# Stick-breaking attention: queries as rows, cumulative sums by a reversed scan

## The chip, the cores and the metric

The kernel runs on one NeuronCore of a Trainium2 chip. The metric is the device time of one execution in microseconds; shown below are the median of three timed runs and one execution taken with the hardware profiler. The engines are TensorE (PE, with its weight loads as PEld), VectorE (DVE), ScalarE (ACT), GpSimd (POOL) and SyncE (SP); TensorE reads SBUF and writes PSUM, an accumulator memory of eight banks, from which VectorE and ScalarE copy. "L955" means line 955 of the kernel before.

## The reference

A two-layer decoder trunk on 512 tokens of width 1024, all float32. Layer 0 mixes a gated linear recurrence with forgetting attention, layer 1 a recurrent branch (Griffin: causal convolution, gates, RG-LRU) with stick-breaking attention. After each mixer stand a residual with LayerNorm, a SwiGLU feed-forward and a second LayerNorm. The change is in the stick-breaking attention of layer 1: 8 heads of 64, blocks of 128 queries.

```python
z = einsum('bqhd,bkhd->bhqk', q_block, k[:, :q1]) * scale
mask = kpos < qpos                                    # strictly causal
log_one_minus = where(mask, log_sigmoid(-z), 0.0)
suffix = cumsum(log_one_minus, axis=3, reverse=True) - log_one_minus
log_w = log_sigmoid(z) + suffix
w = where(mask, exp(log_w), 0.0)
out = einsum('bhqk,bkhd->bqhd', w, v[:, :q1])
```

So each weight needs a sum over all later keys of the same query. With softplus(z) = -log_sigmoid(-z), and since log_sigmoid(z) = z - softplus(z), a weight is exp(z minus the sum of softplus over this key and all later allowed ones).

## The kernel before

Large products are made to nearly float32 accuracy out of three float32r products: each operand is split into a high part (a ScalarE copy) and a low part (a VectorE subtraction), and `mm3` (L256 to L258) issues high by high, high by low and low by high. `weights` (L238 to L246) loads a 128x1024 weight block over SP's queue and splits it; `proj` runs one block of a projection, 24 matmuls of 512 columns, into one of two PSUM banks with the tag "g"; `put` (L251, L252) splits a result.

The order is not written by hand. The kernel is traced in program order, and a planner orders the instructions of each engine by priority and its own costs, assigns buffers of a tag in turn, and inserts semaphores; each engine then runs its queue in order. `high_priority` moves weight splits ahead, `issue_after` and `behind` add an order between two instructions.

Layer 1 (`layer1`) runs the recurrent branch (`griffin`), the value projection, and then four times `sb_pair`, each for two heads e = 0, 1. After the last pair is traced, `out_rows(yc, S_WO1)` runs the half of the output projection that needs only the recurrent branch; the other half follows in the next phase with all four pairs' results.

`qk_pair` projects queries and keys of a pair, head 0 on partitions 0 to 63 and head 1 on 64 to 127. A head's tile holds its high part on its own half of the partitions; on the other half the queries hold their low part (L732), and the keys a second copy of the high part, which VectorE casts out of PSUM (L737). With the low part of the keys in `kz` (L738, zero on the other half), two products give the scores to three terms: q high and low by k high, and q high by k low.

`sb_pair` has keys as rows: for each key block j it computes scores of all queries from block j on, with k as stationary and q as moving operand, and adds a mask by a third product with `sbmask`. The 8 blocks of a pair (2 heads, j = 0 to 3, 512 - 128 j queries wide) are packed into five tiles of 512 columns. Per tile:

- ScalarE copies the scores out of PSUM (L937), VectorE clips them (L938), ScalarE takes exp and ln(1 + x) (L939, L940), VectorE the maximum with z (L941): softplus.
- The softplus is split for TensorE: high part `sh` (L943), low part `sl` (L944).
- The sum over later keys runs down the partitions, so TensorE makes it (L955): `ntri` (-1 on and below the diagonal) sums within the key block, `none` (all -1) adds the later key blocks of the same head, each for `sh` and `sl`, into one bank.
- VectorE adds scores and sums (L957), ScalarE takes the exponential (L958). Keys are rows, so the weights are the moving operand of the value products (L966) as they stand.

A pair has 34 products L955 and 16 products L966. Tags and their numbers of buffers: z 6, l 4, sh 5, sl 5, qk 7. `griffin` uses buffers of sh for its input gates and of sl for its GeLU gates before the pairs need them.

For comparison, `fox_pair` in layer 0 already has queries as rows, transposes its weights on TensorE and stores them in a tile `pT`.

Of the kernel before, what the change touches and what calls it, by code (L numbers as in the profile page):

```python
# [15 lines left out]
P = 128  # L16
# [40 lines left out]
class Trunk:  # L57
    def __init__(self, tc, ctx, ins, out):
# [7 lines left out]
        tile_("fill", [P, 64])  # L66
# [7 lines left out]
        tile_("ntri", [P, P], F32R)  # L74
        tile_("none", [P, P], F32R)
# [640 lines left out]
    def qk_pair(self, iq, ik, low, high=None):  # L716
# [18 lines left out]
        for e, d in enumerate(hv):  # L735
            nc.scalar.copy(ks[e][d], kp[d])
            nc.vector.tensor_copy(ks[e][hv[1 - e]], kp[d])  # L737
            nc.vector.tensor_tensor(low[e][d], kp[d], ks[e][d].bitcast(F32), ALU.subtract)  # L738
# [87 lines left out]
    def griffin(self, xr):  # L826
# [29 lines left out]
        st = []  # L856
        for j in range(4):
# [14 lines left out]
            ig = self.t2k("ig", tag="sh")  # L872
# [4 lines left out]
        gts = []  # L877
        for j in range(4):
            ps = self.proj(S_GR + j)
            g = self.t2k("gt", tag="sl")  # L880
            A(g, ps, AF.Gelu_apprx_tanh)
            gi = self.newest()
            gts.append(g)
# [4 lines left out]
        for j in range(4):  # L888
# [18 lines left out]
            nc.vector.tensor_tensor(ix, ix, gts[j], ALU.mult)  # L907
# [6 lines left out]
    def sb_pair(self, hp, v):  # L914
# [6 lines left out]
        tiles = (((0, 3, 384), (0, 1, 0)), ((1, 3, 384), (1, 1, 0)), ((0, 2, 0), (1, 2, 256)), ((0, 0, 0),), ((1, 0, 0),))  # L921
        sp = {}
        for parts in tiles:
            z, l = self.t2k("z", tag="z"), self.t2k("l", tag="l")
            for e in (0, 1):
                mine = [p for p in parts if p[0] == e]
                if not mine:
                    continue
                ps = self.bank("s", "z")
                for _, j, o in mine:  # L930
                    n = T - j * P
                    b = slice(j * P, j * P + P)
# [4 lines left out]
                nc.scalar.copy(z[:, c], ps[:, c])  # L937
# [4 lines left out]
            sh, sl = self.t2k("sh", dt=F32R, tag="sh"), self.t2k("sl", dt=F32R, tag="sl")  # L942
            nc.scalar.copy(sh, l)  # L943
            nc.vector.tensor_tensor(sl, l, sh.bitcast(F32), ALU.subtract)  # L944
            for e, j, o in parts:
                sp[e, j] = (sh, sl, o)
            sp[parts] = z
        for ti, parts in enumerate(tiles):
            z = sp[parts]
            ps = self.bank(("pt", "po")[ti % 2], "cu")  # L950
            lo = [(self.none, sp[e, i], o + (i - j) * P, T - i * P) for e, j, o in parts for i in range(j + 1, NTB)]
            mms = [(self.ntri, sp[parts[0][:2]][:2] + (0,), 0, T)] + lo
            for n, (w, (sh, sl, oi), c, m) in enumerate(mms):
                for x in (sh, sl):
                    nc.tensor.matmul(ps[:, c:c + m], w, x[:, oi:oi + m], start=n == 0 and x is sh,  # L955
                                     stop=n == len(mms) - 1 and x is sl)
            nc.vector.tensor_tensor(z, z, ps, ALU.add)  # L957
            A(z, z, AF.Exp)  # L958
            ex = self.newest()

        at = {(e, j): (sp[parts], o) for parts in tiles for e, j, o in parts}
        for j in range(NTB):
            for e in range(2):
                h = 2 * hp + e
                z, o = at[e, j]
                nc.tensor.matmul(po[64 * e:64 * e + 64, j * P:T], v[j][:, h * 64:h * 64 + 64], z[:, o:o + T - j * P],  # L966
                                 start=j == 0, stop=j == NTB - 1)
                if j == 0 and e == 0:
                    self.behind(self.newest(), ex)
# [3 lines left out]
    def layer1(self, xr):  # L973
# [3 lines left out]
        for e in range(2):  # L977
            self.nc.gpsimd.memset(self.kz[e][64 - 64 * e:P - 64 * e].bitcast(F32), 0.0)
        yc = self.griffin(xr)
# [13 lines left out]
def hybrid_trunk_kernel(ctx: ExitStack, tc: tile.TileContext, out, **ins):  # L993
# [9 lines left out]
    with t.phase("l1", v=4, qk=7, kz=2, z=6, l=4, sh=5, sl=5) as t.ph:  # L1003
# [38 lines left out]
def layout(inp):  # L1042
# [40 lines left out]
    cst = np.zeros((P, 4, P), f)  # L1083
    cst[:, 0, :] = np.eye(P)
    cst[:, 1, :] = np.where(r[None, :] > r[:, None], -1e30, 0)
    cst[:, 2, :] = np.where(r[:, None] >= r[None, :], -1e30, 0)
    cst[:, 3, :] = np.where(r[:, None] >= r[None, :], -1, 0)
# [25 lines left out]
```

## Time and profile before

| | us |
|---|---|
| median of 3 runs (1236.01 to 1238.81) | 1237.58 |
| the profiled execution | 1234.23 |
| its span, first to last instruction | 1232.5 |
| TensorE busy / weight loads | 1211.2 / 984.2 |
| VectorE busy | 760.5 |
| ScalarE busy | 522.3 |
| GpSimd busy | 66.1 |
| mean granted TensorE clock | 0.995 |

Times in rows of the profile are microseconds from the start of the span unless marked ns. A group's row gives line, engine, operation, "out<-in" by tile names, shapes, count, then busy time with the mean of one, and the idle time of that engine just before with what ended most of it. In the order of time a row is start, recorded length, instruction. [...] A wait's row gives who waited for whom: total, times, longest.

### The profile page before, as it was taken

Reading aid. Unit: us, or ns where it says so; the run is one execution under the profiler, and the core shown is the slowest. Engines: PE = TensorE matmul, PEld = TensorE weight load, DVE = VectorE, ACT = ScalarE, POOL = GpSimd, SP = SyncE. Lnnn points to the kernel's source line nnn. Section 1 sums busy time; section 2 is a strip of 40 time slices with the busy share of each in tenths; the row PEclk is TensorE's granted clock in tenths of the full one; section 3 lists DMA queues with packets and bytes.
Section 4 is the critical chain, followed back from the end, with each engine's and each line's share of the span. In section 5 each row is a group of like instructions: output and inputs, shape, how many; then the busy total and the mean of one; then the engine's idle time right before and its main releaser. Section 6 shows DMA issues by size and latency. Waiting matters only on the chain.

```text
span 1232.5 us, 15454 instructions
## 1 busy us (share of the span) xinstructions
PE 1211.2 (98%) x6119; PEld 984.2 (80%) x6119; DVE 760.5 (62%) x1157; ACT 522.3 (42%) x794; POOL 66.1 (5%) x81
## 2 busy tenths in 40 slices
PE   9999999999999999999999998999999999999997
PEld 6787777679888888888889776777988888888886
DVE  7638789769355635464387597686844554456346
ACT  7447567433233323332233757683333433333220
POOL 2000000000002000200000000000000200020001
PEclk9999999999999999999999999999999999999999
DMA  6421211134637433742324231102554643374321
GB/s 243 154 71 51 86 53 52 52 120 123 219 86 120 137 99 89 119 133 90 103 88 135 69 88 50 45 25 86 157 188 99 103 144 96 91 115 137 103 69 69
DMA packets 45895, 128.03 MB, mean 104 GB/s; under 512 B 4592, under 2 KB 6000, under 8 KB 45824
## 3 DMA queue, kind: packets, MB, share of 16 engines
q1 hardware_dynamic: 35568, 108.51, 27.6%
q0 software_dynamic: 8960, 16.81, 8.6%
q10 hardware_dynamic: 1296, 1.73, 0.4%
q8 instruction: 48, 0.79, 0.3%
q14 instruction: 23, 0.19, 0.1%
HBM read 124.90 MB, written 2.10 MB: 103 GB/s over the span
## 4 chain that ended last, share of the span: by engine, by line
PE 90%; DVE 6%; ACT 2%; DMA 1%; issue 1%; SPq 0%; DVEq 0%; ACTq 0%
PE pf L257 13%; PE pf L256 13%; PE pf L258 13%; PE pj L257 5%; PE pj L256 5%; PE pj L258 5%; PE po L258 4%; PE po L256 4%; PE po L257 4%; PE fa L256 2%; PE fa L258 2%; PE fa L257 2%; PE sc L643 1%; PE fc L258 1%; PE fc L257 1%; PE fc L256 1%
## 5 line engine op out<-in xcount | busy, mean ns | idle before, releaser
L245 ACT CAST wh<-ws 128x1024 fp32r<-128x1024 f32 x143 | 150.2, 1051 | 309.1 <-PE pf L257 119.1
L246 DVE TENSOR_TENSOR wl<-ws,wh 128x1024 fp32r<-128x1024 f32 x143 | 174.9, 1223 | 155.2 <-ACT wh L245 150.4
L256 PE MATMUL pf<-xh,wh 128*128 128x512 f32 x640 | 249.0, 389 | 0.0
L257 PE MATMUL pf<-xl,wh 128*128 128x512 f32 x640 | 249.0, 389 | 0.0
L258 PE MATMUL pf<-xh,wl 128*128 128x512 f32 x640 | 249.0, 389 | 0.0
L257 PEld LDWEIGHTS pf<-xl,wh 128*128 128x128 f32 x640 | 120.1, 188 | 25.1
L258 PEld LDWEIGHTS pf<-xh,wl 128*128 128x128 f32 x640 | 120.1, 188 | 24.9
L256 PEld LDWEIGHTS pf<-xh,wh 128*128 128x128 f32 x640 | 120.1, 188 | 24.7
L533 DVE TENSOR_TENSOR s<-s,pf 128x512 f32<-128x512 f32 x44 | 30.3, 688 | 147.9 <-PE pf L258 147.9
L256 PE MATMUL pj<-xh,wh 128*128 128x512 f32 x256 | 104.2, 407 | 1.0 <-DVE qk L732 0.9
L257 PE MATMUL pj<-xl,wh 128*128 128x512 f32 x256 | 103.6, 405 | 0.2 <-DVE xl L252 0.2
L258 PE MATMUL pj<-xh,wl 128*128 128x512 f32 x256 | 103.8, 405 | 0.0
L251 ACT CAST wh<-wwah 128x1024 fp32r<-128x1024 f32 x32 | 33.7, 1054 | 74.9 <-PE pf L257 63.3
L256 PEld LDWEIGHTS pj<-xh,wh 128*128 128x128 f32 x256 | 48.4, 189 | 12.2 <-PE pj L258 1.8
L257 PEld LDWEIGHTS pj<-xl,wh 128*128 128x128 f32 x256 | 48.4, 189 | 10.2 <-issue 1.1
L258 PEld LDWEIGHTS pj<-xh,wl 128*128 128x128 f32 x256 | 48.4, 189 | 10.1 <-issue 1.6
L256 PE MATMUL po<-wh,yh 128*128 128x512 f32 x128 | 51.4, 402 | 0.0
L258 PE MATMUL po<-wh,yl 128*128 128x512 f32 x128 | 51.1, 399 | 0.0
L257 PE MATMUL po<-wl,yh 128*128 128x512 f32 x128 | 50.8, 397 | 0.0
L252 DVE TENSOR_TENSOR wl<-wwah,wh 128x1024 fp32r<-128x1024 f32 x32 | 38.7, 1220 | 18.5 <-ACT wh L251 17.9
L256 PE MATMUL fa<-wh,fm 128*128 128x512 f32 x128 | 49.9, 390 | 0.0
L257 PE MATMUL fa<-wl,fm 128*128 128x512 f32 x128 | 49.8, 389 | 0.0
(281 smaller groups left out, 2304.6 us busy)
## 6 DMA issues: line engine op xcount, KB each, us to landing
ws<-in_wst SPq DMA_DIRECT2D x165, 512.0 KB, 3.5
wwah<-in_wst POOLq DMA_DIRECT2D x24, 512.0 KB, 5.9
gb<-in_lnp SPq DMA_DIRECT2D x8, 512.0 KB, 4.6
wwah<-in_wst SPq DMA_DIRECT2D x8, 512.0 KB, 6.3
wwal<-in_wst SPq DMA_DIRECT2D x8, 512.0 KB, 7.6
wwal<-in_wst POOLq DMA_DIRECT2D x8, 512.0 KB, 6.7
ws<-in_wst SPq DMA_DIRECT2D x11, 256.0 KB, 5.2
xt<-in_xT SPq DMA_DIRECT2D x8, 256.0 KB, 5.3
```

The lines of the kernel that those rows point to most:

```text
L245: nc.scalar.copy(hi, st)
L246: nc.vector.tensor_tensor(lo, st, hi.bitcast(F32), ALU.subtract)
L251: self.nc.scalar.copy(hi, dst)
L252: self.nc.vector.tensor_tensor(lo, dst, hi.bitcast(F32), ALU.subtract)
L256: mm(ps, ah, bh, start=first, stop=False, **kw)
L257: mm(ps, ah, bl, start=False, stop=False, **kw)
L258: mm(ps, al, bh, start=False, stop=last, **kw)
L533: nc.vector.tensor_tensor(h, h, pb, ALU.mult)
L643: nc.tensor.matmul(ps[u:u + 64, g * 256 + c * 64:g * 256 + (c + 1) * 64], E[:, c * P + u:c * P + u + 64], rhs, start=True, stop=True)
```

## The change

`sb_pair` now has queries as rows. For each query block i of a head it computes the scores against all keys up to block i, with q as stationary and k as moving operand; the mask constant is transposed to match. Again 8 blocks of a pair (128 to 512 keys wide) fill five tiles of 512 columns, each now in one bank with one copy.

- The later keys of a query now lie along the free axis. VectorE makes the sum by a scan over the softplus, through a view that runs backwards (`rev`), in place, one scan per block. The split into `sh` and `sl`, the products with `ntri` and `none`, and both constants go.
- VectorE subtracts the sum from the scores (SBUF from SBUF), ScalarE takes the exponential.
- The values need keys as rows, so TensorE transposes each 128x128 block of weights, 20 a pair, into one of two banks (tags "pt" and "po" in turn), and ScalarE copies them into a tile `pT` of 20 x 128 columns, one copy per block row. All value products come last; `behind` orders them after the newest copy.
- In `qk_pair` the second copy of the keys' high part is made in layer 1 by a transfer from SBUF to SBUF on GpSimd's queue, from ScalarE's copy, where VectorE's cast L737 stood. Layer 0 keeps the cast.
- `griffin` puts its four input gates into one tile and its four GeLU gates into another, both with the new tag pT (2 buffers), which the pairs' `pT` uses later. z has 5 buffers in place of 6; a tile of ones is added for the scan; `fill` grows by what the two constants took.

```diff
-        cst = self.sb.tile([P, 4, P], F32, tag="gb", bufs=1, name="cst")
+        cst = self.sb.tile([P, 3, P], F32, tag="gb", bufs=1, name="cst")
-        cp_(self.ntri, cst[:, 3, :])
-        nc.gpsimd.tensor_scalar(self.none, cst[:, 3, :], 0.0, -1.0, ALU.mult, ALU.add)
...
             nc.scalar.copy(ks[e][d], kp[d])
-            nc.vector.tensor_copy(ks[e][hv[1 - e]], kp[d])
+            if self.qk4:
+                nc.vector.tensor_copy(ks[e][hv[1 - e]], kp[d])
+            else:
+                nc.gpsimd.dma_start(ks[e][hv[1 - e]].bitcast(F32), ks[e][d].bitcast(F32))
             nc.vector.tensor_tensor(low[e][d], kp[d], ks[e][d].bitcast(F32), ALU.subtract)
...
+        igs, gts = [self.t2k("ig", [P, 20 * P], tag="pT") for _ in range(2)]
...
-            ig = self.t2k("ig", tag="sh")
+            ig = igs[:, j * T:(j + 1) * T]
...
-            g = self.t2k("gt", tag="sl")
-            A(g, ps, AF.Gelu_apprx_tanh)
+            A(gts[:, j * T:(j + 1) * T], ps, AF.Gelu_apprx_tanh)
...
-        tiles = (((0, 3, 384), (0, 1, 0)), ((1, 3, 384), (1, 1, 0)), ((0, 2, 0), (1, 2, 256)), ((0, 0, 0),), ((1, 0, 0),))
+        tiles = (((0, 3, 0),), ((1, 3, 0),), ((0, 2, 0), (0, 0, 384)), ((1, 2, 0), (1, 0, 384)), ((0, 1, 0), (1, 1, 256)))
+        pT = self.t2k("pT", [P, 20 * P], tag="pT")
+        at = ((15, -6), (1, 5))
+        rev = lambda a: a[:, ::-1]
...
-                    nc.tensor.matmul(ps[:, o:o + n], k[e][:, b], q[e][:, j * P:T], start=True, stop=False)
-                    nc.tensor.matmul(ps[:, o:o + n], self.kz[e][:, b], q[e][:, j * P:T], start=False, stop=False)
-                    nc.tensor.matmul(ps[:, o:o + P], self.identb, self.sbmask, start=False, stop=True)
-                c = slice(min(p[2] for p in mine), max(p[2] + T - p[1] * P for p in mine))
-                nc.scalar.copy(z[:, c], ps[:, c])
+                nc.tensor.matmul(ps[:, o:o + n], q[e][:, c], k[e][:, 0:n], start=True, stop=False)
+                nc.tensor.matmul(ps[:, o:o + n], q[e][:, c], self.kz[e][:, 0:n], start=False, stop=False)
+                nc.tensor.matmul(ps[:, o + i * P:o + n], self.identb, self.sbmask, start=False, stop=True)
+            nc.scalar.copy(z, ps)
...
-            sh, sl = self.t2k("sh", dt=F32R, tag="sh"), self.t2k("sl", dt=F32R, tag="sl")
-            nc.scalar.copy(sh, l)
-            nc.vector.tensor_tensor(sl, l, sh.bitcast(F32), ALU.subtract)
...
-            lo = [(self.none, sp[e, i], o + (i - j) * P, T - i * P) for e, j, o in parts for i in range(j + 1, NTB)]
-            mms = [(self.ntri, sp[parts[0][:2]][:2] + (0,), 0, T)] + lo
-            for n, (w, (sh, sl, oi), c, m) in enumerate(mms):
-                for x in (sh, sl):
-                    nc.tensor.matmul(ps[:, c:c + m], w, x[:, oi:oi + m], start=n == 0 and x is sh,
-                                     stop=n == len(mms) - 1 and x is sl)
-            nc.vector.tensor_tensor(z, z, ps, ALU.add)
+            for e, i, o in parts:
+                r = rev(l[:, o:o + (i + 1) * P])
+                nc.vector.tensor_tensor_scan(r, self.ones1[:, 0:(i + 1) * P], r, 0.0, ALU.mult, ALU.add)
+            nc.vector.tensor_tensor(z, z, l, ALU.subtract)
             A(z, z, AF.Exp)
-            ex = self.newest()
+            pt = self.bank(("pt", "po")[ti % 2], "pt")
+            for e, i, o in parts:
+                b, step = at[e]
+                for j in range(i + 1):
+                    m = j if step > 0 else i - j
+                    nc.tensor.transpose(pt[:, o + m * P:o + (m + 1) * P], z[:, o + j * P:o + (j + 1) * P], self.ident)
+            for e, i, o in parts:
+                b, step = at[e]
+                lo = b + i + (0 if step > 0 else i * step)
+                dst = bass.AP(tensor=pT.tensor, offset=pT.offset + lo * P,
+                              ap=[pT.ap[0], [abs(step) * P, i + 1], [1, P]])
+                nc.scalar.copy(dst, pt[:, o:o + (i + 1) * P].rearrange("p (j t) -> p j t", t=P))
+        cp = self.newest()
...
-                nc.tensor.matmul(po[64 * e:64 * e + 64, j * P:T], v[j][:, h * 64:h * 64 + 64], z[:, o:o + T - j * P],
+                nc.tensor.matmul(po[64 * e:64 * e + 64, j * P:T], v[j][:, h * 64:h * 64 + 64], pT[:, x:x + T - j * P],
...
-    with t.phase("l1", v=4, qk=7, kz=2, z=6, l=4, sh=5, sl=5) as t.ph:
+    with t.phase("l1", v=4, qk=7, kz=2, z=5, l=4, pT=2, one=1) as t.ph:
```

More of the change, by code (lines that the diff above doesn't have):

```diff
@@ L73, in __init__ @@
             tile_(n, [P, P], BF16)
-        tile_("ntri", [P, P], F32R)
-        tile_("none", [P, P], F32R)
         self.sm = ctx.enter_context(tc.tile_pool(name="sm", bufs=1))
@@ L919, in sb_pair @@
         po = self.bank("ho", "po")
-        tiles = (((0, 3, 384), (0, 1, 0)), ((1, 3, 384), (1, 1, 0)), ((0, 2, 0), (1, 2, 256)), ((0, 0, 0),), ((1, 0, 0),))
-        sp = {}
-        for parts in tiles:
-            z, l = self.t2k("z", tag="z"), self.t2k("l", tag="l")
[L925 to L932, printed above, removed]
-                    nc.tensor.matmul(ps[:, o:o + n], k[e][:, b], q[e][:, j * P:T], start=True, stop=False)
-                    nc.tensor.matmul(ps[:, o:o + n], self.kz[e][:, b], q[e][:, j * P:T], start=False, stop=False)
-                    nc.tensor.matmul(ps[:, o:o + P], self.identb, self.sbmask, start=False, stop=True)
-                c = slice(min(p[2] for p in mine), max(p[2] + T - p[1] * P for p in mine))
-                nc.scalar.copy(z[:, c], ps[:, c])
+        tiles = (((0, 3, 0),), ((1, 3, 0),), ((0, 2, 0), (0, 0, 384)), ((1, 2, 0), (1, 0, 384)), ((0, 1, 0), (1, 1, 256)))
+        pT = self.t2k("pT", [P, 20 * P], tag="pT")
+        at = ((15, -6), (1, 5))
+        rev = lambda a: a[:, ::-1]
+        for ti, parts in enumerate(tiles):
+            z, l = self.t2k("z", tag="z"), self.t2k("l", tag="l")
+            ps = self.bank("s", "z")
+            for e, i, o in parts:
+                n = (i + 1) * P
+                c = slice(i * P, n)
+                nc.tensor.matmul(ps[:, o:o + n], q[e][:, c], k[e][:, 0:n], start=True, stop=False)
+                nc.tensor.matmul(ps[:, o:o + n], q[e][:, c], self.kz[e][:, 0:n], start=False, stop=False)
+                nc.tensor.matmul(ps[:, o + i * P:o + n], self.identb, self.sbmask, start=False, stop=True)
+            nc.scalar.copy(z, ps)
             nc.vector.tensor_scalar(l, z, EXP_MAX, None, ALU.min)
@@ L941, in sb_pair @@
             nc.vector.tensor_tensor(l, l, z, ALU.max)
[L942 to L961 removed]
+            for e, i, o in parts:
+                r = rev(l[:, o:o + (i + 1) * P])
+                nc.vector.tensor_tensor_scan(r, self.ones1[:, 0:(i + 1) * P], r, 0.0, ALU.mult, ALU.add)
+            nc.vector.tensor_tensor(z, z, l, ALU.subtract)
+            A(z, z, AF.Exp)
+            pt = self.bank(("pt", "po")[ti % 2], "pt")
[4 more added lines that the diff above has]
+                    nc.tensor.transpose(pt[:, o + m * P:o + (m + 1) * P], z[:, o + j * P:o + (j + 1) * P], self.ident)
+            for e, i, o in parts:
+                b, step = at[e]
[4 more added lines that the diff above has]
+        cp = self.newest()
         for j in range(NTB):
@@ L978, in layer1 @@
             self.nc.gpsimd.memset(self.kz[e][64 - 64 * e:P - 64 * e].bitcast(F32), 0.0)
+        self.ones1 = self.t2k("ones", tag="one")
+        self.nc.gpsimd.memset(self.ones1, 1.0)
         yc = self.griffin(xr)
@@ L1082, in layout @@
     r = np.arange(P)
-    cst = np.zeros((P, 4, P), f)
+    cst = np.zeros((P, 3, P), f)
     cst[:, 0, :] = np.eye(P)
     cst[:, 1, :] = np.where(r[None, :] > r[:, None], -1e30, 0)
-    cst[:, 2, :] = np.where(r[:, None] >= r[None, :], -1e30, 0)
-    cst[:, 3, :] = np.where(r[:, None] >= r[None, :], -1, 0)
+    cst[:, 2, :] = np.where(r[None, :] >= r[:, None], -1e30, 0)
     o["cst"] = cst
```

10 lines of the change are left out of this document (4 added, 6 removed).

## The prediction

> **What bounds the kernel now.** I read the page first (busy times, chain of waits), then the stretch in which layer 1 works its four pairs of stick-breaking heads (737 to 836.5 us of the span), by windows, by waits and in order of time.
>
> ```profile
> PE 1211.2 (98%) x6119; PEld 984.2 (80%) x6119; DVE 760.5 (62%) x1157; ACT 522.3 (42%) x794; POOL 66.1 (5%) x81
> PE 90%; DVE 6%; ACT 2%; DMA 1%; issue 1%; SPq 0%; DVEq 0%; ACTq 0%
> ```
>
> TensorE carries 90% of the chain that ends last. Its busy share overstates it, since the recorded matmuls overlap (0.39 us long, a new one every 0.23 us), so TensorE work is priced below by start-to-start distances. Next, the windows: stretch, length, then busy us of PE, PEld, DVE, ACT, POOL, granted clock, DMA. The first four rows are the four pairs, cut where a pair's value products begin or end; the fifth is their sum; the last two are a piece of the first pair.
>
> ```profile
> 737.00:762.10 25.10, 20.69 (x99) 15.98 (x99) 19.65 (x32) 18.24 (x33) 0.00 (x0) 0.93 0.25 82
> 762.10:785.00 22.90, 22.35 (x115) 16.88 (x114) 15.83 (x26) 16.83 (x31) 0.00 (x0) 1.00 0.08 24
> 785.00:812.60 27.60, 26.37 (x133) 19.39 (x132) 20.31 (x32) 20.62 (x37) 0.00 (x0) 1.00 0.13 39
> 812.60:836.50 23.90, 23.74 (x126) 17.41 (x125) 17.23 (x28) 16.34 (x29) 0.00 (x0) 1.00 0.08 23
> 737.00:836.50 99.50, 93.15 (x470) 69.66 (x470) 73.02 (x116) 72.03 (x127) 0.00 (x0) 0.98 0.14 42
> 750.00:757.10 7.10, 3.65 (x20) 2.56 (x19) 5.99 (x10) 6.15 (x12) 0.00 (x0) 0.98 0.24 75
> 757.10:760.30 3.20, 3.20 (x10) 2.91 (x11) 2.41 (x4) 1.11 (x2) 0.00 (x0) 0.51 0.00 0
> ```
>
> TensorE is the bound in the last three pairs (idle 0.55, 1.23 and 0.16 us). In the first it is not: it idles 4.4 us there, and then runs 3.2 us at 0.51 of its clock, another 1.6 us lost. Together the stretch loses 6.35 + 1.6 = 8.0 us. What ended those waits:
>
> ```profile
> PE cu L955 <- DVE z L957: 4.7, 7, 2.4
> PEld cu L955 <- DVE z L957: 4.2, 4, 2.5
> ```
>
> It is VectorE: the cumulative sums wait for their PSUM bank, which VectorE's addition L957 empties late. VectorE is at 19.65 of 25.10 us there, a share of 0.78. So the reader should see two limits, TensorE and close behind it VectorE; the change takes from the first and gives to the second.
>
> **TensorE: products removed, transposes added.** The last pair runs its cumulative sums densely (start, recorded length, instruction):
>
> ```profile
> 822.80 0.39 PE L955 MATMUL cu<-sh,ntri 128*128 128x512 f32 x1
> 823.03 0.39 PE L257 MATMUL po<-wl,yh 128*128 128x512 f32 x1
> ...
> 826.25 0.40 PE L955 MATMUL cu<-sh,none 128*128 128x256 f32 x2
> 826.48 0.40 PE L258 MATMUL po<-wh,yl 128*128 128x512 f32 x1
> ...
> 827.18 0.28 PE L955 MATMUL cu<-sl,none 128*128 128x256 f32 x1
> 827.81 0.44 PE L258 MATMUL po<-wh,yl 128*128 128x512 f32 x1
> ...
> 828.69 0.51 PE L955 MATMUL cu<-sh,ntri 128*128 128x512 f32 x1
> 829.55 0.27 PE L955 MATMUL cu<-sl,none 128*128 128x128 f32 x1
> ...
> 829.98 0.47 PE L955 MATMUL cu<-sh,ntri 128*128 128x512 f32 x1 [0.16 <-DVE z L957]
> 831.29 0.45 PE L955 MATMUL cu<-sh,ntri 128*128 128x512 f32 x1
> 832.58 0.45 PE L258 MATMUL po<-wh,yl 128*128 128x512 f32 x1
> ```
>
> Tiles 1 and 2: four 512-column products at 0.23 (0.92) and eight smaller ones (0.23 + 0.63 = 0.86). Tile 3: six in 0.86 plus about 0.1 for the last, 0.97. Tiles 4 and 5: 1.31 and 1.29. That is 5.35 us a pair, 21.4 us in four. A transpose of 128x128 f32 is seen in the layer norm, eight of them before the next product starts:
>
> ```profile
> 858.51 1.23 PE L323 MATMUL tr<-ident,xt 128*128 128x128 f32 x8
> 859.50 0.48 PE L256 MATMUL po<-wh,yh 128*128 128x512 f32 x1
> ```
>
> 0.99 / 8 = 0.124 us each; 20 a pair, 80 in all, 9.9 us. The score products swap stationary and moving operand but keep counts and widths (8 blocks of 128 to 512 columns, twice, plus 8 masks), and the 16 value products a pair keep theirs: nothing. TensorE's work falls by 21.4 - 9.9 = **11.5 us**.
>
> **VectorE: two operations out, scans in.** Groups (count | busy, mean ns):
>
> ```profile
> L944 DVE TENSOR_TENSOR sl<-l,sh 128x512 fp32r<-128x512 f32 x20 | 13.5, 686 | 0.9 <-ACT sh L943 0.9
> L737 DVE CAST qk<-pj 64x512 fp32r<-64x512 f32 x16 | 11.0, 689 | 3.5 <-ACT qk L736 3.2
> L906 DVE TENSOR_TENSOR_SCAN ig<-w,ig 128x512 f32<-128x512 f32 x4 | 4.9, 1221 | 0.1
> L569 DVE TENSOR_TENSOR_SCAN bb<-ones,bb 128x128 f32<-128x128 f32 x16 | 5.9, 408 | 0.0
> ```
>
> Out: the 20 low parts (13.5 us) and the 8 key casts of layer 1 (half of the 16, 5.5 us). In: per pair scans of 512, 384, 256 and 128 columns, two of each. The rows at both ends give a straight line of (1221 - 408) / 384 = 2.12 ns a column, so 1.22 + 0.95 + 0.68 + 0.41, twice, 6.5 us a pair, 26.1 in all. The subtraction that replaces L957 is the same size; nothing. VectorE **gains 7.1 us**: 73.0 becomes 80.1. No row shows a scan over a reversed view. I take the forward price; at a cycle saved per column it would be half (-13 us), at a doubled one +26 us. Nothing in the trace speaks for either end, and both stay in the range.
>
> **ScalarE: copies swapped.**
>
> ```profile
> L943 ACT CAST sh<-l 128x512 fp32r<-128x512 f32 x20 | 12.1, 619 | 0.5 <-DVE l L941 0.4
> L937 ACT COPY z<-z x24: 354/582/594, 739.7 to 821.3; 128x512 f32<-128x512 f32 x16, 128x256 f32<-128x256 f32 x8
> ```
>
> Out: 20 high parts, 12.1 us, and four score copies (16 x 0.58 + 8 x 0.354 becomes 20 x 0.58: -0.5). In: eight copies of transposed weights a pair out of PSUM, two each of 512, 384, 256, 128 columns, by the line between 0.354 and 0.582 some 0.58 + 0.47 + 0.35 + 0.24, twice, 3.3 us, 13.2 in all. Net +0.6 us: nothing, below VectorE's load. New wait: such a copy waits for its transposes, and behind it on ScalarE stand the exponentials of later tiles; before, the exponential L958 waited for VectorE at the same place, so I charge none.
>
> **The key copy.** The projected keys of pair 0:
>
> ```profile
> 735.96 0.58 ACT L736 CAST qk<-pj 64x512 fp32r<-64x512 f32 x1
> 737.23 0.68 DVE L737 CAST qk<-pj 64x512 fp32r<-64x512 f32 x1
> ...
> 739.27 0.69 DVE L737 CAST qk<-pj 64x512 fp32r<-64x512 f32 x1 [0.65 <-ACT qk L736]
> ```
>
> and the transfers of POOL's queue (size, median us from issue to landing):
>
> ```profile
> k<-c POOLq DMA_DIRECT2D x8, 4.0 KB, 1.6
> wwah<-in_wst POOLq DMA_DIRECT2D x24, 512.0 KB, 5.9
> ```
>
> The new transfer is 64 rows of 2 KB, 128 KB: between 1.6 and 5.9 us; by size, 1.6 + 4.3 x 128/512 = 2.7. It starts when ScalarE's copy ends (736.5) and lands at 739.2, where the cast ended at 737.9: **1.3 us later** in pair 0. In the later pairs the cast itself waited for VectorE, so I charge nothing there. If the transfer takes 5.9, it is 4.5 in pair 0 and 3.2 more in each other pair. POOL has nothing else in these stretches (0.00 busy above), so nothing queues behind it.
>
> [...]
>
> ```profile
> L938 DVE TENSOR_SCALAR l<-z 128x512 f32<-128x512 f32 x20 | 8.2, 422 | 2.5 <-ACT z L937 2.4
> ```
>
> **Edits at nothing.** Gates and inputs of the recurrent branch become slices of two tiles, which the first pairs' transposed weights reuse. The work that hides this is the scores of pair 0: the branch's last write starts at 735.37, and transposes come no earlier than a chain of score, softplus and scan after 737. Without that cover the copies would wait for it. The smaller constant load and two POOL operations fewer lie in layer 0 and POOL has no share in the chain. Five score tiles in place of six: a score tile is now free after its transposes, not after the value products; nothing or a gain.
>
> ```profile
> 735.37 0.69 DVE L252 TENSOR_TENSOR yl<-ig,yh 128x512 fp32r<-128x512 f32 x1
> L332 DVE SCALAR_TENSOR_TENSOR xt<-xt,po x8: 678/686/689, 820.3 to 850.0; 128x512 f32<-128x512 f32 x8
> L251 ACT CAST yh<-po x2: 586/586/586, 815.5 to 836.6; 128x512 fp32r<-128x512 f32 x2
> L252 DVE TENSOR_TENSOR yl<-po,yh x2: 692/692/692, 816.2 to 837.2; 128x512 fp32r<-128x512 f32 x2
> ```
>
> **The sum.** The first half of the output projection needs only the recurrent branch, so it fills TensorE while the last pair finishes; its last addition starts at 850.0 (L332 above), 13.5 us after the last value products (836.5). The second half needs the last pair, whose result takes 0.59 + 0.69 = 1.3 us to be split (L251, L252). So the second half starts at the later of two times. TensorE alone: 849.9 - 11.5 = 838.4, if it still loses 8.0 us. The pairs: VectorE's 80.1 us at the share of 0.78, the one measured where it was the limit, take 102.7 us, 3.2 more than 99.5; with the key's 1.3 the last value products end at 841.0, plus 1.3 is 842.3. The pairs decide: 849.9 - 842.3 = **7.6 us gained**. The profiled execution took 1234.23 us around a span of 1232.5, so it would take 1226.6; the median of the runs shown, 1237.58, lies 3.35 above it, and from it I predict **1230.0**. Its own range is a gain of 4 to 10, 1227 to 1234.
>
> [...]
>
> **Rivals.**
> 1. *TensorE stays the bound.* Tiles no longer depend on each other (before, the first key block's sum needed all later blocks), and score tiles free early, so VectorE could run denser. From a share of 80.1 / (837.1 - 737 - 1.3) = 0.81 on, all 11.5 us come: 1226. For: the four pairs would share VectorE work. Against: 0.78 was all it reached under pressure. Chance 0.25.
> 2. *The first pair's stall goes too*, 3.4 of its 4.4 us of waits and 1.6 of clock: a gain of 16.5, 1221. For: L957's bank wait is gone. Against: scans are heavier than what they replace. Chance 0.07.
> 3. *No change: VectorE takes over.* At the share of before, 73.02 / 99.5 = 0.73, 80.1 us take 109.1; with key and split the second half starts at 848.7: a gain of 1.2, 1236.4. For: three engines would then have about equal loads. Against: 0.73 was reached without need. Chance 0.12.
> 4. *Slower: the key transfer is late in every pair.* Score products wait in TensorE's queue with projections behind them. At 5.9 us instead of 2.7 each pair loses 3.2, 12.8 in all: 7.6 - 12.8 = -5.2, 1242.8. It decides from a landing of about 4.6 us. For: weights of 512 KB share the engines. Against: 0.08 to 0.25 DMA share in these stretches. [...] Chance 0.14, a slow reversed scan included.
>
> **Numbers.** Forecast 0.42. A change under 0.2% (2.5 us) can't be told from none. Faster: forecast, rivals 1 and 2, 0.74; same: rival 3, 0.12; slower: rival 4, 0.14. The range 1220 to 1241 holds rivals 1 to 3 and reaches toward the fourth.
>
> **What would show it.** Right: no cumulative-sum products; 80 transposes at 0.12 us start to start; scans at 1.2 us for 512 columns; VectorE about 80 us busy between the first scores and the last value products, a stretch near 104 us; the first half of the output projection done before it ends, then a wait of TensorE on VectorE or on the last transposes. Wrong: scans at another price, keys landing later than 3 us, score products as the longest waits of TensorE, or a stretch well under 100 us.

## The result: slower by half a per cent, and the profile after

The changed kernel takes 1243.48 us (median of four runs, 1240.06 to 1245.76) against 1237.39 for the kernel before beside it: a ratio of 1.0049, 95% interval 1.0031 to 1.0068. It is 6 us slower where 7.6 us faster was forecast. The profiled execution took 1240.06 us around a span of 1238.3 (before: 1234.23 around 1232.5). Line numbers below are those of the kernel whose profile is shown; edits move them by a few lines.

The page of the changed kernel, busy times and chain of waits:

```profile
PE 1200.1 (97%) x6063; PEld 972.7 (79%) x6063; DVE 764.9 (62%) x1161; ACT 522.8 (42%) x802; POOL 69.9 (6%) x88
PE 82%; DVE 9%; ACT 4%; DMA 4%; issue 1%; SPq 0%; POOL 0%; DVEq 0%; ACTq 0%; POOLq 0%
```

TensorE has 11.1 us less to do, nearly the 11.5 forecast, and yet its share of the chain that ends last falls from 90% to 82%: others hold it up more often. Groups of the new operations (count | busy, mean ns of one | idle before):

```profile
L939 DVE TENSOR_TENSOR_SCAN l<-ones,l 128x512 f32<-128x512 f32 x8 | 9.8, 1220 | 0.1
L939 DVE TENSOR_TENSOR_SCAN l<-ones,l 128x384 f32<-128x384 f32 x8 | 7.6, 947 | 0.1
L939 DVE TENSOR_TENSOR_SCAN l<-ones,l 128x256 f32<-128x256 f32 x8 | 5.2, 681 | 0.1
L939 DVE TENSOR_TENSOR_SCAN l<-ones,l 128x128 f32<-128x128 f32 x8 | 3.2, 402 | 0.0
L948 PE MATMUL pt<-ident,z 128*128 128x128 f32 x80 | 13.8, 298 | 10.4 <-ACT z L941 10.3
```

The scans cost what the straight line said (25.8 us in all, forecast 26.1); their view that runs backwards costs nothing (1220 ns at 512 columns, 1222 for the forward scan of the recurrent branch in the same profile). So the prices of the operations are not where the forecast went wrong. The same 123 us of both kernels, by windows (stretch, length, busy us of PE, PEld, DVE, ACT, POOL, granted clock, DMA); first before, then after:

```profile
737.00:860.00 123.00, 116.65 (x575) 88.87 (x576) 88.54 (x138) 79.74 (x136) 0.92 (x1) 0.99 0.18 56
```

```profile
737.00:860.00 123.00, 102.01 (x502) 74.98 (x501) 90.60 (x135) 79.52 (x143) 4.26 (x8) 0.96 0.22 62
```

TensorE's idle time in this stretch rises from 6.35 to 20.99 us. Over the whole span, less the busy time, it rises from 21.3 to 38.2: 16.9 us more idle against 11.1 less busy make the 5.8 by which the profiled execution is longer. The lower clock, 0.96 in place of 0.99, does not come on top, since matmuls at a lower clock count longer in the busy time (a product L253 of 512 columns is recorded with 0.39 us at a clock of 1.00 and with 0.63 between 759.70 and 765.00 us, where the clock is 0.50). Taken from windows of half a microsecond, as busy time times the share of clock that was missing, it costs 3.9 us in place of 1.6. The waits of TensorE in the stretch from 725 to 860 us (who waited for whom: total, times, longest):

```profile
PE pt L948 <- ACT z L941: 10.3, 10, 2.9
PE pj L252 <- DVE qk L728: 4.8, 3, 2.7
PE z L929 <- DMA qk<-qk: 4.2, 2, 3.0
PE po L252 <- DVE qk L728: 2.1, 1, 2.1
```

Four candidates: the transposes wait for the exponential; the next products of a projection, and of the output projection, wait for the operation that empties the queries out of PSUM (L728); and the scores wait for the new key transfer. The worst place, in order of time on TensorE (start, recorded length, instruction, in brackets the idle time before it):

```profile
744.24 0.40 PE L254 MATMUL pj<-xh,wl 128*128 128x512 f32 x1
744.47 0.39 PE L252 MATMUL pj<-xh,wh 128*128 128x512 f32 x1
...
753.94 0.47 PE L254 MATMUL pj<-xh,wl 128*128 128x512 f32 x1
757.34 0.66 PE L948 MATMUL pt<-ident,z 128*128 128x128 f32 x4 [2.93 <-ACT z L941]
759.78 1.11 PE L948 MATMUL pt<-ident,z 128*128 128x128 f32 x4 [1.78 <-ACT z L941]
761.84 0.80 PE L252 MATMUL pj<-xh,wh 128*128 128x512 f32 x1 [0.94 <-DVE qk L728]
```

The reader should count the projection products (pj). From 744.47 to 753.94 there are 24, one whole projection: the keys of the second pair. The product at 744.24 ends the queries before it, so their bank is complete at 744.64. After 753.94 the next projection needs a bank again, and gets it only at 761.84. In between TensorE has nothing but four transposes at a time. The operations that empty the queries' bank, on VectorE and, ahead of it, on ScalarE, in order of time in the same profile:

```profile
755.96 0.66 DVE L940 TENSOR_TENSOR z<-z,l 128x512 f32<-128x512 f32 x1
759.04 0.68 DVE L728 SCALAR_TENSOR_TENSOR qk<-pj,qk 64x512 fp32r<-64x512 f32 x1
761.09 0.69 DVE L728 SCALAR_TENSOR_TENSOR qk<-pj,qk 64x512 fp32r<-64x512 f32 x1
```

```profile
754.79 0.59 ACT L954 COPY pT<-pt 128x512 f32<-128x512 f32 x1
756.66 0.63 ACT L941 ACTIVATE z<-z 128x512 f32<-128x512 f32 x1 [1.28 <-DVE z L940]
757.20 0.57 ACT L725 ACTIVATE qk<-pj 64x512 fp32r<-64x512 f32 x1
760.36 0.59 ACT L725 ACTIVATE qk<-pj 64x512 fp32r<-64x512 f32 x1
```

The bank was complete at 744.64, and ScalarE's first copy out of it (L725) starts at 757.20, behind a copy of transposed weights and an exponential that waits for VectorE. Nor was ScalarE idle until then: from 749.00 to 754.40 it was busy for 5.14 of 5.40 us, with the first pair's tiles for the most part. VectorE's second subtraction ends at 761.78, and 0.06 us later TensorE starts. Before the exponential at 756.66 ScalarE idles 1.28 us, while this copy, whose bank is complete since 744.64 and which could have run some 12 us earlier, stands behind it: in these rows ScalarE works its queue in order.

### The profile page after: what moved, and what is told of

Same layout as the page of the kernel before. It is cut to its first block, busy times and chain, and to the rows that moved or that the text cites. A ratio compares the mean times of both kernels' runs of the same rounds, so it can differ in the third digit from the quotient of the medians.

```text
span 1238.3 us, 15379 instructions
## 1 busy us (share of the span) xinstructions
PE 1200.1 (97%) x6063; PEld 972.7 (79%) x6063; DVE 764.9 (62%) x1161; ACT 522.8 (42%) x802; POOL 69.9 (6%) x88
## 4 chain that ended last, share of the span: by engine, by line
PE 82%; DVE 9%; ACT 4%; DMA 4%; issue 1%; SPq 0%; POOL 0%; DVEq 0%; ACTq 0%; POOLq 0%
PE pf L253 13%; PE pf L252 13%; PE pf L254 13%; PE pj L252 4%; PE pj L253 4%; PE pj L254 4%; PE po L252 3%; PE po L254 3%; PE po L253 3%; PE fa L252 2%; PE fa L254 2%; PE fa L253 2%; DMA ws<-in_wst 2%; DVE l L939 2%; PE sc L639 1%
## 5 line engine op out<-in xcount | busy, mean ns | idle before, releaser
L242 DVE TENSOR_TENSOR wl<-ws,wh 128x1024 fp32r<-128x1024 f32 x143 | 174.8, 1222 | 150.5 <-ACT wh L241 147.0
L253 PE MATMUL pf<-xl,wh 128*128 128x512 f32 x640 | 249.0, 389 | 0.0
L253 PEld LDWEIGHTS pf<-xl,wh 128*128 128x128 f32 x640 | 120.2, 188 | 24.9
L253 PE MATMUL pj<-xl,wh 128*128 128x512 f32 x256 | 104.1, 406 | 0.3 <-DVE xl L248 0.2
L253 PEld LDWEIGHTS pj<-xl,wh 128*128 128x128 f32 x256 | 48.9, 191 | 10.3 <-issue 1.0
L253 PE MATMUL po<-wl,yh 128*128 128x512 f32 x128 | 51.0, 399 | 0.0
L432 POOL DMA_DIRECT2D wwah<-in_wst x24 | 29.0, 1208 | 387.3 <-DVE wl L248 367.1
L248 DVE TENSOR_TENSOR wl<-wwah,wh 128x1024 fp32r<-128x1024 f32 x32 | 38.7, 1220 | 18.2 <-ACT wh L247 17.8
```

The costliest lines, as they stand in the source:

```text
L242: nc.vector.tensor_tensor(lo, st, hi.bitcast(F32), ALU.subtract)
L248: self.nc.vector.tensor_tensor(lo, dst, hi.bitcast(F32), ALU.subtract)
L253: mm(ps, ah, bl, start=False, stop=False, **kw)
L432: nc.gpsimd.dma_start(dst, src, accum_op=ALU.add)
```

## The experiments

Four theories stand behind the expectations: **K**, the key transfer comes late; **V**, VectorE has too much to do; **Q**, the transposes stand at a bad place in TensorE's queue, ahead of work that could run; **O**, the emptying of the projections stands too late in order (first thought of as VectorE's, behind the scans). Each ratio is to the kernel before on the same chip, with its 95% interval.

### e1_cast and e2_before_key: the key transfer alone

The first takes the transfer back out of the changed kernel, the second puts it alone into the kernel before:

```diff
-            if self.qk4:
-                nc.vector.tensor_copy(ks[e][hv[1 - e]], kp[d])
-            else:
-                nc.gpsimd.dma_start(ks[e][hv[1 - e]].bitcast(F32), ks[e][d].bitcast(F32))
+            nc.vector.tensor_copy(ks[e][hv[1 - e]], kp[d])
```

> The changed kernel with the key copy done again by VectorE's cast. If the late key transfer is what cost the time (theory K: TensorE waited 3.0 and 1.2 us for it, and lost clock after the first), 4 to 7 us come back: ratio to the kernel before about 1.000. If VectorE's load is the cause (theory V), 5.5 us of casts are added to the engine that sets the pace: the same time as the changed kernel or up to 4 us more, ratio 1.005 to 1.008. If the place of the transposes in TensorE's queue is the cause (theory Q), little moves: within 3 us of the changed kernel.

> The kernel before with one part of the change alone: the second key copy by a transfer on GpSimd's queue. Theory K: slower than before by 3 to 6 us, ratio 1.003 to 1.005. Theories V and Q: no change or up to 2 us faster, since VectorE loses 5.5 us of casts.

Measured: e1_cast 1243.74 us, 1.0046 (1.0034 to 1.0058), as slow as the changed kernel; e2_before_key 1236.68 us, 0.9992 (0.9983 to 1.0001), the kernel before. K falls from both sides, in this sense: each run exchanges the transfer for the cast or the cast for the transfer, and the exchange costs nothing. That is so although the transfer is late: the first score product of the changed kernel, in order of time, against 737.96 in the kernel before. The expectation was also wrong that clock was lost after this wait; the window from 742 to 745 us (last section) has 1.00.

```profile
742.64 0.47 PE L929 MATMUL z<-qk,qk 128*128 128x512 f32 x1 [3.04 <-DMA qk<-qk]
```

### e3_noscan: the scans left out

```diff
-            for e, i, o in parts:
-                r = rev(l[:, o:o + (i + 1) * P])
-                nc.vector.tensor_tensor_scan(r, self.ones1[:, 0:(i + 1) * P], r, 0.0, ALU.mult, ALU.add)
```

> The changed kernel without the scans: the cumulative sums over later keys are left out, all else is as it was. Takes 26.1 us from VectorE. Theory V: most of TensorE's 20.7 us of waits in the pairs goes, 15 us or more faster than the changed kernel, ratio to before below 0.993. Theory Q: the chain of a tile is a scan shorter, but the planner places the transposes earlier too, so the waits on the exponential stay: 3 to 8 us faster, ratio 0.998 to 1.003.

Measured: 1230.2 us, 0.9944 (0.9931 to 0.9957), 13 us below the changed kernel for 25.8 us of scans, between the two cases of the expectation. In its trace TensorE's wait for the exponential falls from 10.3 to 1.4 us, while its waits for the emptied queries stay (7.3 us after 6.9). The scans' part in the loss is real, but this run can't tell the amount of VectorE's work from the length of the chain: a scan that is gone also shortens every chain.

### e4_late1: the transposes of a tile behind the exponential of the next

```diff
+            exps.append(self.newest())
+            zs.append((z, ti, parts))
+        for z, ti, parts in zs:
...
+                    if first and ti + 1 < len(tiles):
+                        self.behind(self.newest(), exps[ti + 1])
```

> The changed kernel with a tile's transposes traced after all five tiles and ordered behind the exponential of the next tile, with no work added or removed. Theory Q: TensorE's waits on the exponential (10.3 us in the pairs) fall below 4 us and 5 to 10 us come back, ratio to before 0.996 to 1.001. Theory V: VectorE sets the pace whatever TensorE's order is, so the time stays within 2 us of the changed kernel, ratio 1.004 to 1.006.

Measured: 1244.48 us, 1.0051 (1.0035 to 1.0067): nothing won. TensorE's waits in the stretch from 725 to 860 us:

```profile
PE pj L252 <- DVE qk L728: 9.9, 3, 5.1
PE po L252 <- DVE qk L728: 4.6, 1, 4.6
PE pt L953 <- ACT z L942: 4.1, 4, 3.0
```

The transposes' wait fell from 10.3 to 4.1 us, and the wait for the emptied queries (L728) rose from 6.9 to 14.5. So the wait has only changed its name: TensorE lacks work because the queries' bank is not free, whatever instruction stands first in its queue. Q falls as the main cause, and the row that grew names the next suspect.

### e5_qkfirst and e8_before_qkfirst: the emptying of queries and keys drawn forward

The block around the operations that empty both projections makes the planner treat them as if they had been written 600 places earlier; in e5_qkfirst in the changed kernel, in e8_before_qkfirst in the kernel before. For the queries (the keys' block is alike):

```diff
-        for e, d in enumerate(hv):
-            nc.scalar.mul(qs[e][d], qp[d], 0.125)
...
-            nc.vector.scalar_tensor_tensor(qs[e][hv[1 - e]], qp[d], 0.125, qs[e][d].bitcast(F32), ALU.mult,
-                                           ALU.subtract)
+        with self.tc.high_priority(offset=0 if self.qk4 else 600):
+            for e, d in enumerate(hv):
+                nc.scalar.mul(qs[e][d], qp[d], 0.125)
...
+                nc.vector.scalar_tensor_tensor(qs[e][hv[1 - e]], qp[d], 0.125, qs[e][d].bitcast(F32), ALU.mult,
+                                               ALU.subtract)
```

> The changed kernel with the planner's priority raised for the four operations that empty the projections of queries and keys out of PSUM, in layer 1; no work added or removed. Theory O (order on VectorE: the emptying of the projections stands behind a pair's scans in VectorE's queue, so TensorE has no bank for the next projection, waits, and runs at half clock afterwards): TensorE's waits on L728 go, the next pair's scores overlap with this pair's scans, 8 to 14 us come back, ratio to the kernel before 0.993 to 0.999. Theory V (VectorE's total in the pairs is the bound): the same 80 us of VectorE work in the same order of length, within 2 us of the changed kernel, ratio 1.003 to 1.006.

> The kernel before with the same raised priority for emptying the projections in layer 1. If what the priority gives belongs to the change's heavier VectorE chain (theory O), the kernel before, whose TensorE waited 0.9 us on that operation, gains at most 3 us: ratio 0.998 to 1.001. If the raised priority is simply a better plan for any kernel (a rival to theory O), it gains here as much as in the changed kernel.

Measured: e5_qkfirst 1225.45 us, 0.9908 (0.9894 to 0.9921), 18 us below the changed kernel with the same operations, more than the 8 to 14 that O had let expect. TensorE's waits in the stretch from 725 to 860 us:

```profile
PE pt L950 <- ACT z L943: 5.7, 10, 1.0
PE z L931 <- DMA qk<-qk: 3.0, 2, 2.5
PE pj L252 <- DVE qk L729: 1.2, 1, 1.2
```

From 737 us to the end of the last addition of the output projection's first half, first the changed kernel, then e5_qkfirst:

```profile
737.00:856.10 119.10, 98.15 (x485) 71.80 (x483) 87.44 (x131) 78.63 (x142) 4.26 (x8) 0.96 0.20 58
```

```profile
737.00:841.70 104.70, 94.73 (x481) 69.40 (x480) 86.30 (x130) 76.81 (x142) 4.25 (x8) 0.98 0.22 66
```

VectorE does nearly the same work (86.30 against 87.44 us busy) in 14.4 us less: in the changed kernel it was not full, it was waiting too. O holds, V as a bound over the whole stretch falls. But e8_before_qkfirst, 1230.02 us, 0.9953 (0.9937 to 0.9969), wins 7 us where at most 3 were expected: drawing this emptying forward helps the kernel before too. So not all of the 18 us were brought by the change.

### e6_minpool and e7_qkfirst_minpool: less work for VectorE

The clip moves to GpSimd, alone and together with the edit of e5_qkfirst:

```diff
-            nc.vector.tensor_scalar(l, z, EXP_MAX, None, ALU.min)
+            nc.gpsimd.tensor_scalar(l, z, EXP_MAX, None, ALU.min)
```

> The changed kernel with the clip of the scores (20 times 0.42 us) moved from VectorE to GpSimd. Theory V: 8.3 us less on VectorE, 5 us or more faster than the changed kernel, ratio to before below 1.001. Theory O: the clip's way over GpSimd lengthens every tile's chain and the projections are emptied no earlier: within 3 us of the changed kernel, or slower, ratio 1.003 to 1.010.

> Both of the two together. Theory O: about the time of the priority alone, within 3 us. Theory V: 5 us or more faster than the priority alone.

Measured: e6_minpool 1247.14 us, 1.0081 (1.0067 to 1.0096); e7_qkfirst_minpool 1231.82 us, 0.9957 (0.9942 to 0.9972). Both are slower than without the edit, by 4 and 6 us, although 8.3 us of clips leave VectorE; O had allowed 3 us for the second. The clips' group in e6_minpool:

```profile
L933 POOL TENSOR_SCALAR l<-z 128x512 f32<-128x512 f32 x20 | 33.8, 1702 | 37.1 <-ACT z L932 31.6 <-DVE yl L248 5.5
```

One clip takes 1702 ns there (416 on VectorE in the changed kernel, 422 by the row L938 in the prediction), inside the chain of each tile. VectorE is also relieved of less than the clips: beside them its scans of 512 columns take 1434 ns in place of 1220, and by its groups only 4.7 of the 8.3 us are saved. And ScalarE's first copy of the second pair's queries starts at 761.66 us, later still than in the changed kernel (757.20). That the length of a tile's chain counts for more than VectorE's load fits these runs; they do not take the three effects apart.

### e9_q_late1, e10_q_noscan and e12_q_cast: what is left with the order mended

The edits of e4_late1, e3_noscan and e1_cast, each on top of e5_qkfirst.

> The changed kernel with both edits that were tried alone: the projections' emptying drawn forward, and the transposes of a tile placed behind the exponential of the next tile. In the kernel with the emptying drawn forward, TensorE's transposes still waited 5.7 us for the exponentials, spread over ten waits of 1.0 us. If place Q is what remains once the order O is mended, most of these 5.7 us come: 1225.5 - 5 = 1220.5. If those waits only stand where another would (VectorE's row of work is the limit at that point, so the wait moves to the score products or to the value products), the time stays within 2 us of 1225.5. If the later transposes delay the value products of a pair and with them the next pair's, it is 2 to 4 us slower.

> The changed kernel with the emptying drawn forward and without its scans: the cumulative sums are left out, everything else is done. It takes 26 us from VectorE in these stretches. By O (the scans hurt only because the emptying of the projections stood behind them) little is left to win here: 1225.5 to about 1222, the 3 us being part of the transposes' waits, which follow the scan in the chain of a tile. By V (VectorE's amount of work is the bound whatever the order) the 13 us that leaving the scans out gave without this priority come again, 1212 or so. Between: the transposes' waits of 5.7 us and the clock lost with them come, 1218.

> The changed kernel with the emptying drawn forward and the second key copy made by VectorE's cast again, in place of the transfer. The score products of two pairs waited 2.5 us each for the transfer in the kernel with the emptying drawn forward, 3.0 in all. If these 3 us are on the path that sets the end, the cast wins 1 to 3: 1223 to 1224. If VectorE's time is the dearer of the two (5.5 us more of it, at the place where it is fullest), the cast loses as much: 1226 to 1229. If both are hidden, as the two runs without the priority showed, within 1.2 us of 1225.5.

Measured on one chip, with e11_q_only (below, 1225.87 us) beside them: e9_q_late1 1225.78 us, 0.9919 (0.9904 to 0.9933); e10_q_noscan 1218.12 us, 0.9856 (0.9844 to 0.9869); e12_q_cast 1226.62 us, 0.9928 (0.9916 to 0.9939). The place of the transposes is worth nothing here either, and the cast in place of the transfer gives no gain: 0.75 us slower than e11_q_only beside it, and by the ratios some 2.5 slower than e5_qkfirst, whose edit it shares. (Of the two waits for the transfer in e5_qkfirst one was 2.5 us and the other 0.5, not 2.5 each.) The scans are worth 6 us by the ratio to e5_qkfirst and 8 against e11_q_only on the same chip, near the case "between" of the expectation, down from 13. The transposes' waits of 5.7 us are gone from the trace of e10_q_noscan: the scans lengthen the chain that the transposes wait for. Alone, leaving out the scans and drawing the emptying forward win 13 and 18 us, together 25, so the two losses overlap.

### e11_q_only, e13_q_act and e14_q_dve: which operation, on which engine

The block of e5_qkfirst around the queries' two operations (e11_q_only), around ScalarE's alone (e13_q_act, shown) and around VectorE's alone (e14_q_dve):

```diff
-            nc.scalar.mul(qs[e][d], qp[d], 0.125)
+            with self.tc.high_priority(offset=0 if self.qk4 else 600):
+                nc.scalar.mul(qs[e][d], qp[d], 0.125)
```

> The changed kernel with the emptying of the queries' projection alone drawn forward, the keys' left where the planner had it. The longest waits of the changed kernel that stand behind VectorE's emptying are for the operation that empties the queries (5.1 us in three pairs, where the transposes were moved). If that one operation is the cause, this keeps nearly all of the 18 us: 1226 to 1228. If the keys' two operations matter as much (the score products need both), about half stays: 1234. If the queries' part is nothing by itself: 1243.

> The changed kernel with only ScalarE's half of the queries' emptying (the scaled copy of the high part) drawn forward; VectorE's half (the subtraction that gives the low part, after which the bank is free) stays where the planner puts it. In the changed kernel ScalarE begins the first of these copies of pair 1 at 757.20, behind a copy of transposed weights and an exponential that waited for VectorE, and VectorE ends the second subtraction at 761.8. If ScalarE's queue is what holds the bank, this kernel is as fast as the one with both halves forward: 1226. If VectorE's queue is, the subtraction stays late and the time stays within 3 us of the changed kernel's, 1241 to 1245. If each holds it for a part: 1232 to 1238.

> The changed kernel with only VectorE's half of the queries' emptying drawn forward; ScalarE's half stays. VectorE's subtraction needs ScalarE's copy, so a subtraction placed early on VectorE either drags nothing along (the planner lets it wait until the copy is planned), and the time stays at 1241 to 1245, or stands in VectorE's queue waiting for ScalarE with the scans behind it, and it is slower, 1246 or more. If VectorE's queue alone was the cause (theory O as first put), it is as fast as with both halves forward: 1226.

Measured: e11_q_only 1225.87 us, 0.9921 (0.9908 to 0.9934); e13_q_act 1227.65 us, 0.9923 (0.9908 to 0.9937); e14_q_dve 1236.50 us, 0.9997 (0.9985 to 1.0008). The queries carry the gain, and drawing ScalarE's copy alone forward carries as much as both operations. O as first put, with VectorE's queue as the place, falls: drawing VectorE's half forward wins 6 us of the 15, which none of the three cases of its expectation had. In e13_q_act, on ScalarE and then on VectorE in order of time:

```profile
745.12 1.04 ACT L241 CAST wh<-ws 128x1024 fp32r<-128x1024 f32 x1 [1.23 <-PE pj L253]
746.08 0.59 ACT L726 ACTIVATE qk<-pj 64x512 fp32r<-64x512 f32 x1
...
748.30 0.60 ACT L726 ACTIVATE qk<-pj 64x512 fp32r<-64x512 f32 x1
```

```profile
747.46 0.69 DVE L729 SCALAR_TENSOR_TENSOR qk<-pj,qk 64x512 fp32r<-64x512 f32 x1
749.23 0.69 DVE L729 SCALAR_TENSOR_TENSOR qk<-pj,qk 64x512 fp32r<-64x512 f32 x1
```

ScalarE copies at 746.08 what it copied at 757.20 in the changed kernel, and VectorE, with no priority of its own, is done at 749.92 instead of 761.78. What that gives TensorE, by windows; first the changed kernel, then e13_q_act:

```profile
754.40:765.00 10.60, 4.94 (x17) 3.65 (x17) 9.79 (x16) 7.24 (x15) 0.81 (x2) 0.68 0.23 63
```

```profile
754.40:765.00 10.60, 9.60 (x47) 6.83 (x46) 9.91 (x17) 8.99 (x18) 1.04 (x2) 1.00 0.25 75
```

TensorE has 47 recorded matmuls in place of 17, at full clock. VectorE is as busy in the one as in the other: what the changed kernel lacks here is not VectorE's time but a free bank for the next projection. In e14_q_dve the first copies of the second, third and fourth pair on ScalarE still come late, as in the changed kernel (757.20, 782.76, 809.03), but less and less so; a part of its 6 us can come from that:

```profile
756.77 0.57 ACT L725 ACTIVATE qk<-pj 64x512 fp32r<-64x512 f32 x1
...
777.66 0.59 ACT L725 ACTIVATE qk<-pj 64x512 fp32r<-64x512 f32 x1
...
795.82 0.59 ACT L725 ACTIVATE qk<-pj 64x512 fp32r<-64x512 f32 x1
```

### e15_before_q: the queries alone, in the kernel before

> The kernel before with the queries' emptying alone drawn forward, the twin of the changed kernel with that edit. There all four operations of queries and keys drawn forward gave 0.9953 (7 us); half of the changed kernel's gain was not the change's at all. If the queries' part carries it here too, 0.9953 again, and the change is worth some 4 to 5 us once the queries are emptied in time. If it was the keys' emptying in the kernel before (its score products waited 1.0 us for the cast), little is left, 0.999, and the change with that edit is worth 10 us.

Measured: 1231.45 us, 0.9949 (0.9937 to 0.9961), the first case. On the same chip e13_q_act took 1227.65: with the queries' copy in time, the change is worth 3.8 us, and e5_qkfirst against e8_before_qkfirst gives 4.6. In the kernel before the gain does not stand in the wait for the queries, which is 0.9 us with and without the edit. The cumulative sums' wait for VectorE falls from 4.7 to 1.6 us and the clock stays at 1.00. That projection products come in time to fill those waits would explain it; it is not tested apart.

## Why the prediction was wrong, by its own steps

**What held.** TensorE's term: -11.5 forecast, -11.1 by the page, where 2.3 us more of lost clock are counted in, so the work taken away is somewhat more. Transposes: four between 753.53 and the next product at 753.94, 0.10 us each against 0.124. The scans: 25.8 against 26.1 us. VectorE by its groups: 25.8 - 13.5 - 5.5 = +6.8 against +7.1. (Over all its groups it is +6.4, from 806.5 to 812.9; these add recorded lengths that overlap. The page, which counts an overlap once, has +4.4.) The pairs' term: VectorE's 80.1 us at a share of 0.78, with the last value products ending at 841.0. In the changed kernel, the window up to their end and the products themselves:

```profile
737.00:843.90 106.90, 86.50 (x437) 62.82 (x435) 81.90 (x123) 74.98 (x138) 4.26 (x8) 0.95 0.19 55
```

```profile
841.43 2.48 PE L961 MATMUL po<-pT,v 128*64 128x512 f32 x16
```

They end at 843.9, 2.9 us late, at a share of 81.90 / 106.90 = 0.77. The first score came 3.4 us later than I had it: ScalarE's copy of the keys ended 1.3 us later than in the profile before (737.84 against 736.54), as the queries' first copy already did (730.52 against 729.21), and the key transfer took the other 2.1 (below).

**The step that failed** is in the sum: "TensorE alone: 849.9 - 11.5 = 838.4, if it still loses 8.0 us". The second half of the output projection starts at the later of two times, and I let the pairs decide with 842.3. The last addition of the first half in the changed kernel (850.0 before):

```profile
855.41 0.68 DVE L328 SCALAR_TENSOR_TENSOR xt<-xt,po 128x512 f32<-128x512 f32 x1
```

It is TensorE's side that decides: this addition comes 5.4 us later than before instead of 11.5 earlier, and ends 12.2 us after the last value products, where the prediction named "the first half of the output projection done before it ends" as a sign of being right. TensorE lost 24.9 us, not 8.0 (20.99 idle and 3.9 of clock, before 6.35 and 1.6). I held its losses constant while I lengthened the chain of every tile and took away products that could fill waits; which of the two counts for more, no run takes apart.

**The sentence in which the mechanism was passed over** is the one on the new wait: a copy of transposed weights waits for its transposes, with exponentials behind it, "before, the exponential L958 waited for VectorE at the same place, so I charge none". I named what stands behind on ScalarE and left out the operation that matters: the scaled copy of the next pair's queries, by which a PSUM bank comes free. Shown is that drawing it forward wins the changed kernel some 15 us (e13_q_act); in the kernel before, drawing both of the queries' operations forward wins some 6 (e15_before_q). The 9 to 11 us of difference turn a change worth about 4 us into one that costs 6. Two things stay open. The planner orders all the rest anew after such an edit, so the 15 us belong to the copy's place with what follows from it; no run gives the projections a third bank, which would test the bank by itself. And why the planner placed the copy so late is only argued: its order follows its own costs, which no run shows.

**The key copy** was mis-sized: 2.7 us forecast, median 2.2, but 4.4 us for the first pair, which with the 1.3 us above put the first score at 742.64 where I had 739.2. Exchanged for the cast it made no difference to the time (e1_cast, e2_before_key). Two signs named for being wrong thus came, keys landing later than 3 us and a score product with TensorE's longest single wait, and neither was the cause. Rival 4, slower by this transfer at 1242.8, came within a microsecond of the time, for a reason that fell: the nearness of a number says nothing for its mechanism.

**The clock** stood in the sum with the 1.6 us of before. It took 3.9 - 1.6 = 2.3 us more in the profiled execution. The other three timed ones, 2.5 to 5.7 us longer, had a mean clock of 0.988 to 0.989 in place of 0.994: a lower clock goes with the 3.4 us by which the median lies above the profiled execution.

**What is left** of the 7.6 forecast with the order mended is 4 us. The same 123 us of e15_before_q and of e13_q_act:

```profile
737.00:860.00 123.00, 119.64 (x594) 89.76 (x593) 93.03 (x144) 82.05 (x138) 0.92 (x1) 1.00 0.18 56
```

```profile
737.00:860.00 123.00, 112.00 (x562) 83.95 (x561) 101.32 (x156) 81.93 (x146) 6.10 (x10) 0.97 0.21 64
```

With the copy in time in both, TensorE still idles 11.0 us in the changed kernel against 3.4. e10_q_noscan shows 6 to 8 us of the scans still on the path, although VectorE has idle time: each tile's chain of scores, softplus, scan, subtraction, exponential and transposes is longer by a scan. That a pair's five tiles are too few to fill such a chain's waits is what I would argue; no run varies their number.

The version that beats both kernels is the change with the queries' and keys' emptying drawn forward, e5_qkfirst: 1225.45 us, 0.9908 of the kernel before. e9_q_late1, e11_q_only and e13_q_act are not told apart from it.

## What to carry to other kernels

When a change takes work off the engine that bounds, look at what that engine did in the waits of the others: the removed work may have been their filler, and the time that an engine idles is not constant (TensorE's here: 21.3 us before, 38.2 after). Follow each accumulator bank from its last product to the instruction that empties it, and compare the two times; an operation of half a microsecond that sits late in another engine's queue can cost as much as the new operations, here some 15 us against 13 for the scans. A wait that only changes its name under an edit, as the transposes' did, points to the resource behind both names.

## What the runs showed of the hardware that was not expected

TensorE's clock fell after idle gaps in no simple relation to their length. Windows of 3 us around and after the first score of pair 0, in three kernels: the changed kernel (first score at 742.64, after a wait of 3.04 us), e13_q_act (741.95, after 3.63) and e5_qkfirst (742.22, after 2.54):

```profile
742.00:745.00 3.00, 2.36 (x11) 1.76 (x11) 0.43 (x1) 1.15 (x2) 0.00 (x0) 1.00 0.14 55
```

```profile
742.00:745.00 3.00, 3.00 (x8) 2.09 (x9) 0.43 (x1) 0.59 (x1) 0.00 (x0) 0.50 0.02 7
```

```profile
742.00:745.00 3.00, 2.78 (x8) 1.95 (x9) 0.43 (x1) 0.59 (x1) 0.00 (x0) 0.58 0.25 68
```

After the gap of 3.04 us the clock was 1.00 in its window, after the one of 3.63 us 0.50, and after the one of 2.54 us 0.58. After the two of 2.93 and 1.78 us around 757, with 0.66 us of work between, it was 0.50 from 759.70 to 765.00. What decides, no run here shows.

A scan over a view that runs backwards costs what a forward one does: 1220 against 1222 ns at 512 columns. A transfer of 128 KB inside SBUF landed after 2.1 to 4.4 us in the changed kernel, with a median of 2.2; the longest is that of the first pair, at a DMA share of 0.70 between 737 and 742 us.
